# Expert steps in another order, and all weight subtractions in them on VectorE

## The chip, the cores and the metric

The kernel runs on one core of a Trainium2 chip. The metric is the device time of one launch in microseconds (us), as the median of three runs.

## The reference

A transformer of three layers on 1024 tokens of 1024 features: neighbourhood attention, grouped-query attention, and a hybrid mixer, each followed by a mixture of 32 experts. The changed code computes the experts. Each token goes to two of 32 experts, and an expert is a gated product:

```python
def expert_block(args):
    xb, e = args
    return (jax.nn.silu(xb @ w_gate[e]) * (xb @ w_up[e])) @ w_down[e]
```

The hidden width of an expert is 512 in the first two layers (wide) and 256 in the third (narrow). All inputs are float32, and the results are scaled by the gate and added up per token.

## The kernel before

Each of the three layers ends with a stage that runs its 32 experts in turn, each for its first 128 tokens (class `Experts`). The work is cut into steps; a step is the product with one tile `R` of 1 MB of the weights. In a wide layer an expert has six: g0 and g1 are the gate's product (into `pj` in PSUM), g2 and g3 the up product (into `S`), d0 and d1 the second product (into `O` and `R` in PSUM). In the narrow layer a g step makes both gate and up halves of `pj` for half of the features, so an expert has g0, g1 and one d.

For float32 accuracy each product is made of three on rounded operands (`mm3`, lines 181 to 184): high times high, low times high, high times low. So a tile of weights is split before its use: `make` (line 2189) rounds it on ScalarE to `H` (line 2197) and subtracts on VectorE, or for every sixth tile on GpSimd, to get `L` (line 2198). `make` runs three steps ahead of the product; there are four buffers of `H` and `L`. When a tile is split, `load` (line 2154) has SyncE's queue fetch the tile ten places on into the same buffer; the ring has ten.

Around the products there are small pieces of work per expert, in the methods that the change moves:

- `tokens(e, g)`: four transpositions on TensorE of half of the gathered rows `X` (line 2217) into `tp`, then the two parts `xh` (ScalarE, line 196) and `xl` (VectorE, line 197); after the second half GpSimd issues the gather of a later expert's rows (line 2205).
- `silu(e)`: ScalarE, `a` from `pj` (line 2231). `gated(e)`: VectorE, `a` times the up product (line 2235).
- `hidden(e)`: the transpositions of `a` (line 2217), then `th` and `tl`.
- `done(e)`: VectorE scales the second product out of PSUM (line 2247, two instructions) and GpSimd scatters the rows to `y` (line 2248).

The order of all of it on every engine is written by hand: `run` goes through the list `seq` and calls `step`, within a manual schedule, so each engine executes its instructions in the order in which `step` issues them. In `seq` the second product of an expert stands within the first products of the next: in a wide layer g0, g1 of expert e, then d0, d1 of e - 1, then g2, g3 of e. `gated(e-1)` stands before g0 and `hidden(e-1)` before g1.

Of the kernel before, what the change touches and what calls it, by code (L numbers as in the profile page):

```python
# [22 lines left out]
P = 128  # L23
# [16 lines left out]
def constants():  # L40
    """Arrays that depend on shapes alone."""
# [54 lines left out]
def part(gen, n):  # L96
    """The next n steps of gen."""
    return islice(gen, n)


def mixed(main, side, nm, ns):
    """Both generators to their ends, ns steps of side spread over nm of main."""
    done = 0
    for i, _ in enumerate(main):
        want = (i + 1) * ns // nm
        while done < want:
            done += 1
            next(side, None)
        yield
    run(side)  # L110


def together(gens, n, apart):
    """Steps of up to n generators in turn, to the ends of all; one starts the given steps after another."""
# [9 lines left out]
# the pools of the tiles of the weights of the experts, in turn; the first two hold four other tiles before  # L124
# [11 lines left out]
class K:  # L136
# [19 lines left out]
    # ---------------------------------------------------------------- setup  # L156
# [17 lines left out]
    def log_exp(self, after):  # L174
        """The functions Ln and Exp together, from after the given instruction on."""
        with self.tc.issue_after(after.ins):
            self.nc.scalar.preload_act_table_set("natural_log_exp_and_others")

    # ---------------------------------------------------------------- products
# [6 lines left out]
    def split(self, raw, hi, lo):  # L186
        """hi <- raw rounded to float32r; lo <- the rest."""
# [4 lines left out]
    def evac_split(self, src, hi, lo, scale=None):  # L192
        """hi, lo <- the two parts of src * scale, src in PSUM."""
# [8 lines left out]
    def feature_major(self, src, t, scol, bcol, hh, hl, pool):  # L202
        """Columns t of hh, hl <- the transposed token tile src, scaled and shifted per feature, in steps."""
# [18 lines left out]
    # ---------------------------------------------------------------- modulation  # L222
    def condition(self, c, name):
        """silu(c) over partitions."""
# [4 lines left out]
    def first_rows(self, x, ca, w, b, scol, bcol, hh, hl, q, r, closed):  # L229
        """hh, hl <- the transposed x * s + t per feature, for t, s - 1 <- the first 2048 entries of silu(c) @ w + b.  # L230

        In a first step all that does not need these entries, then by tile; closed() ends the tiles of q."""
# [76 lines left out]
    def modulation(self, ca, w, b, mod, first, last, pool):  # L309
        """Entries 512 * first to 512 * last of mod (DRAM) <- silu(c) @ w + b, in steps, outside TensorE but for the sum over partitions."""  # L310
        nc = self.nc
        todo = [(n, k) for n in range(first, last + 1) for k in range(NK)]
        # the bias of one part comes within the next part
# [18 lines left out]
        def total(acc, n):  # L332
            """The sum over partitions, in steps."""
# [33 lines left out]
    # ---------------------------------------------------------------- between mixer and experts  # L367
    def load_out(self, lay, moe, queue):
        """The next loads for the output product of the mixer, as far as there is room."""
# [13 lines left out]
    def mixer_out(self, lay, x, ot, x1, h2, hi, pool, first, moe, done):  # L383
        """x1 <- norm(alpha * x + (1 + g1) * (o @ w_o)); h2 <- the modulated x1; routes it.

        done() is called when the tiles of the pool first are no longer needed."""
# [30 lines left out]
        # the modulated rows are z * (g * (1 + sc)) + (b * (1 + sc) + sh)  # L417
# [14 lines left out]
        # the router takes the rows before their norm: its weights for them, and what the mean and the shift come to  # L432
# [145 lines left out]
    def columns(self, lay, prev, scol, bcol):  # L578
        """Scale and shift of the normalised rows of layer prev into the input of the mixer of lay."""
# [9 lines left out]
    # ---------------------------------------------------------------- neighbourhood attention  # L589
    def na_tables(self):  # L590
        """DRAM: the bias table of each head with room around it for the masked positions."""
# [13 lines left out]
    def na_attention(self, hh, hl, w, tables, ot, start, started, side):  # L605
        """ot (DRAM, features x tokens) <- the attention of hh + hl (features x tokens) without its output product."""
# [19 lines left out]
        # the parts of the weights of the values lie where other tiles do later  # L626
# [48 lines left out]
        # the products for keys, then queries, of each pair of heads: 16 products in a row  # L675
# [8 lines left out]
        def weights(n, half):  # L684
            """One half of the features of the weights of product n: the high part; the low one of the half before."""
# [11 lines left out]
        def project(j):  # L697
            """Step j: half of the sum over features for half of the tokens of product j // 4."""
# [15 lines left out]
        def settle(lo):  # L714
            """The next head's part of a product that is done, out of PSUM: its high part; then its low part."""
# [33 lines left out]
        def bias(h, ty):  # L749
            """The biases and the mask of head h for windows of type ty."""  # L750
# [15 lines left out]
        def scores(i):  # L766
            """Window i % 4 of head i // 4: the exponentials of its two halves."""
# [118 lines left out]
    # ---------------------------------------------------------------- vectors and norms  # L886
    def row(self, pool, src, name, bufs=1):
        """A vector of DRAM on every partition."""
# [5 lines left out]
    def col(self, pool, src, name):  # L894
        """A vector of DRAM over partitions: element k * 128 + p at (p, k)."""
# [4 lines left out]
    def rsqrt(self, out, v, tmp):  # L900
        """out <- v ** -0.5 (columns), in steps."""
# [8 lines left out]
    def normal(self, out, z, s):  # L910
        """out <- (z - mean) / std over its row, in steps; s: 20 columns that start with the statistics of the halves."""
# [9 lines left out]
    # ---------------------------------------------------------------- mixture of experts  # L921
# [1594 lines left out]
```

## Time and profile before

| | us |
|---|---|
| median of 3 runs | 4152.44 (4148.66 to 4153.31) |
| span of the profiled execution | 4140.5 |
| first wide stage, first product to last scaling, about | 637.7 (726.4 to 1364.1) |
| second wide stage, about | 637.7 (2196.5 to 2834.2) |
| narrow stage, about | 326 (3720 to 4046) |

Of the profiled execution the span is recorded, from its first instruction to its last; its own total time is not recorded apart. The span is 11.9 us under the median. Times in the rows below are us from the start of the span, durations in us unless marked ns. In rows of engines a bracket tells how long the engine was idle before the instruction and what ended that.

### The profile page before, as it was taken

How to read it: one execution, taken by the hardware profiler on the slowest of the kernel's cores; microseconds unless marked ns; L12 is line 12 of the kernel's file. 1: busy time of each engine (PE TensorE's matmuls, PEld its weight loads, DVE VectorE, ACT ScalarE, POOL GpSimd, SP SyncE). 2: the span in 40 equal slices, each digit the busy share in tenths (PEclk: the TensorE clock that was granted, in tenths of full speed). 3: DMA queues.
4: the chain of work that ended last, by engine and by line, in shares of the span. 5: the costliest groups of instructions: out<-in, count | busy, mean ns of one | idle time of the engine just before them, and what ended most of it. 6: DMA issues, size and time to landing. Idle time of an engine off the chain costs nothing. (4 is left out here: it accounts for less than half of the span.)

```text
span 4140.5 us, 51186 instructions
## 1 busy us (share of the span) xinstructions
PE 3457.2 (83%) x17648; PEld 2802.6 (68%) x17648; DVE 3382.8 (82%) x5129; ACT 2293.8 (55%) x3295; POOL 1905.4 (46%) x1230
## 2 busy tenths in 40 slices
PE   5999876899989687999877999984899879769991
PEld 4777665777777476777666777773778767657771
DVE  6599979888888797999797888888465578788986
ACT  3377632666666455888425666664352266227772
POOL 2255425444554234868454445544412142257763
PEclk8999988999999898999998999997999999989996
DMA  8878753999998547434537999995210012649994
GB/s 268 227 147 161 169 165 131 326 346 347 349 342 292 185 134 245 134 118 128 163 130 282 341 337 345 350 346 193 67 39 1 19 56 71 197 154 325 337 347 186
DMA packets 554648, 880.10 MB, mean 213 GB/s; under 512 B 117167, under 2 KB 280623, under 8 KB 551312
## 3 DMA queue, kind: packets, MB, share of 16 engines
q1 hardware_dynamic: 477008, 745.90, 54.1%
q0 software_dynamic: 77376, 130.88, 10.5%
q8 instruction: 141, 2.31, 0.2%
q14 instruction: 123, 1.01, 0.1%
HBM read 791.89 MB, written 126.82 MB: 222 GB/s over the span
## 5 line engine op out<-in xcount | busy, mean ns | idle before, releaser
L2198 DVE TENSOR_TENSOR L<-R,H 128x2048 fp32r<-128x2048 f32 x394 | 1057.0, 2683 | 178.7 <-ACT H L2197 178.7
L2197 ACT ACTIVATE H<-R 128x2048 fp32r<-128x2048 f32 x480 | 918.3, 1914 | 86.8 <-PE S L184 69.5
L2205 POOL DMA_INDIRECT X<-h,slots x87 | 194.8, 2239 | 575.1 <-PE tp L2217 554.8
L2198 POOL TENSOR_TENSOR L<-R,H 128x2048 fp32r<-128x2048 f32 x86 | 398.3, 4632 | 104.4 <-ACT H L2197 95.0
L182 PE MATMUL pj<-H,xh 128*128 128x512 f32 x776 | 319.4, 412 | 2.5 <-ACT H L188 2.5
L183 PE MATMUL pj<-L,xh 128*128 128x512 f32 x776 | 307.1, 396 | 1.8 <-DVE L L189 1.8
L184 PE MATMUL pj<-H,xl 128*128 128x512 f32 x776 | 307.6, 396 | 0.0
L2248 POOL DMA_INDIRECT y<-O,slots x96 | 263.8, 2747 | 92.9 <-DVE O L2247 57.7
L360 POOL TENSOR_TENSOR macc<-macc,mw 128x512 f32<-128x512 f32 x182 | 237.5, 1305 | 72.6 <-ACT mw L356 63.1
L196 ACT ACTIVATE ph<-tp 128x512 fp32r<-128x512 f32 (+1 forms) x352 | 199.4, 567 | 115.5 <-PE tp L1225 102.3
L197 DVE TENSOR_TENSOR pl<-tp,ph 128x512 fp32r<-128x512 f32 (+1 forms) x352 | 224.7, 645 | 25.0 <-ACT ph L196 23.6
L196 ACT ACTIVATE xh<-tp 128x512 fp32r<-128x512 f32 x194 | 116.0, 599 | 189.1 <-PE tp L2217 146.4
L1209 DVE TENSOR_REDUCE st<-S 128x1 f32<-128x1024 f32 (+2 forms) x192 | 204.1, 1063 | 19.2 <-PE S L1515 16.2
L182 PE MATMUL S<-H,xh 128*128 128x512 f32 x512 | 204.7, 400 | 0.0
L184 PE MATMUL S<-H,xl 128*128 128x512 f32 x512 | 200.5, 392 | 0.0
L183 PE MATMUL S<-L,xh 128*128 128x512 f32 x512 | 200.3, 391 | 0.0
L196 ACT ACTIVATE th<-tp 128x512 fp32r<-128x512 f32 (+1 forms) x97 | 51.0, 526 | 249.2 <-PE tp L2217 248.1
L1225 PE MATMUL tp<-ident,E 128*128 128x128 f32 x1111 | 171.5, 272 | 0.5 <-DVE pl L197 0.5
L1236 PE MATMUL O<-ph,V 128*128 128x512 f32 (+1 forms) x352 | 162.9, 463 | 10.4 <-DVE U L1243 10.4
L184 PEld LDWEIGHTS pj<-H,xl 128*128 128x128 f32 x776 | 148.0, 191 | 33.5 <-DVE xl L197 0.7
L182 PEld LDWEIGHTS pj<-H,xh 128*128 128x128 f32 x776 | 149.1, 192 | 30.8 <-ACT H L188 2.8
L183 PEld LDWEIGHTS pj<-L,xh 128*128 128x128 f32 x776 | 149.0, 192 | 30.2 <-DVE L L189 2.1
(589 smaller groups left out, 10198.3 us busy)
## 6 DMA issues: line engine op xcount, KB each, us to landing
R<-moe_w_down SPq DMA_DIRECT2D x161, 1024.0 KB
R<-moe_w_up SPq DMA_DIRECT2D x127, 1024.0 KB
R<-moe_w_gate SPq DMA_DIRECT2D x126, 1024.0 KB
mw<-ada_w SPq DMA_DIRECT2D x160, 256.0 KB
R<-moe_w_gate SPq DMA_DIRECT2D x66, 512.0 KB
R<-moe_w_up SPq DMA_DIRECT2D x66, 512.0 KB
Y<-y SPq DMA_DIRECT2D x24, 1024.0 KB
mw<-w_mod SPq DMA_DIRECT2D x96, 256.0 KB
```

The costliest lines, as they stand in the source:

```text
L182: mm(out, ah, bh, start=first, stop=False)
L183: mm(out, ah, bl, start=False, stop=False)
L184: mm(out, al, bh, start=False, stop=last)
L196: nc.scalar.activation(hi, src, AF.Copy)
L197: nc.vector.tensor_sub(lo, src, hi.bitcast(F32))
L360: nc.gpsimd.tensor_add(acc, acc, W)
L1209: nc.vector.tensor_reduce(blk.st[:, a, 0:1], S[:, :n], axis=AX.X, op=ALU.max, negate=True)
L1225: nc.tensor.transpose(tp[:, a, :], blk.E[a][:, c * P:(c + 1) * P], self.ident)
L2197: self.nc.scalar.activation(hi, r, AF.Copy)
L2198: (engine or (self.nc.gpsimd if i % 6 == 5 and i < self.n - 4 else self.nc.vector)).tensor_sub(lo, r, hi.bitcast(F32))
L2205: return self.nc.gpsimd.indirect_dma_start(out=self.X[e % 3], out_offset=None, in_=self.h2d, in_offset=IOA(ap=i, axis=0), bounds_check=T - ...
L2248: ins = nc.gpsimd.indirect_dma_start(out=self.y, out_offset=IOA(ap=self.slots.bitcast(I32)[:, 1, e:e + 1], axis=0), in_=O, in_offset=None, ...
```

## The change

Four things, all within the experts' steps.

- `seq`: the first products of an expert are no longer split by the second product of another. In a wide layer g0 to g3 of expert e are followed by d0, d1 of e - 1; in the narrow layer g0, g1 of expert e by d of e - 2.
- The small pieces stand at other steps. Wide: `hidden(e-1)` and `done(e-2)` before g1, `tokens(e+1, 0)` before g2, `silu(e)` and `tokens(e+1, 1)` before g3, `gated(e)` before d1. So three steps lie between the up product and the transposition of `a`, where there was one, and three between that and the second product, where there was one. Narrow: `silu(e-1)`, `gated(e-1)`, `tokens(e+1, 0)`, `done(e-3)` before g0, `tokens(e+1, 1)` before g1, `hidden(e-1)` before d.
- All subtractions that `step` causes are VectorE's. Those of three tiles per layer that are made before the stage name GpSimd themselves and stay there.
- Comments and docstrings are taken out, which moves line numbers by two in this part (2198 becomes 2196, 2217 becomes 2215, 2235 becomes 2233).

```diff
-        for e in range(33):
-            down = [("d", e - 1, j) for j in range(self.NF // 2)]
...
-            self.seq += up[0] + (down if e else []) + up[1]
+        lag = 1 if self.FF == 512 else 2
+        for e in range(32 + lag):
+            if e < 32:
+                self.seq += [("g", e, j) for j in range(self.FF // 128)]
+            if e >= lag:
+                self.seq += [("d", e - lag, j) for j in range(self.NF // 2)]
...
-        (engine or (self.nc.gpsimd if i % 6 == 5 and i < self.n - 4 else self.nc.vector)).tensor_sub(lo, r, hi.bitcast(F32))
+        (engine or self.nc.vector).tensor_sub(lo, r, hi.bitcast(F32))
...
+    def wide(self, kind, e, j):
+        if kind == "g":
+            if j == 0:
+                self.acc[e] = [self.k.ps.tile([P, 512], F32, name=n, bufs=2) for n in ("pj", "S")]
+                if e == 1:
+                    self.gated(0)
+            elif j == 1:
+                if e:
+                    self.hidden(e - 1)
+                if e > 1:
+                    self.done(e - 2)
+            elif j == 2:
+                self.tokens(e + 1, 0)
+            else:
+                self.silu(e)
+                self.tokens(e + 1, 1)
+        else:
+            if j == 0:
+                if e == 31:
+                    self.done(30)
+                    self.hidden(31)
+                self.out[e] = [self.k.ps.tile([P, 512], F32, name=n, bufs=1) for n in "OR"]
+            elif e < 31:
+                self.gated(e + 1)
+
+    def narrow(self, kind, e, j):
+        if kind == "g":
+            if j == 0:
+                self.acc[e] = [self.k.ps.tile([P, 512], F32, name="pj", bufs=2)]
+                if e:
+                    self.silu(e - 1)
+                    self.gated(e - 1)
+                self.tokens(e + 1, 0)
+                if e > 2:
+                    self.done(e - 3)
+            else:
+                self.tokens(e + 1, 1)
+                if e == 1:
+                    self.hidden(0)
+        else:
+            if e > 29:
+                self.done(e - 1)
+            self.out[e] = [self.k.ps.tile([P, 512], F32, name=n, bufs=1) for n in "OR"]
+            if e == 29:
+                self.silu(31)
+                self.gated(31)
+            if e < 31:
+                self.hidden(e + 1)
...
+        (self.wide if self.FF == 512 else self.narrow)(kind, e, j)
```

Three places show the new order. First VectorE in the middle of a wide stage, one expert and its repetition's start, before:

```order
L2235 TENSOR_TENSOR a<-S,a 128x512
L2198 TENSOR_TENSOR L<-R,H 128x2048
L197 TENSOR_TENSOR tl<-tp,th 128x512
L2198 TENSOR_TENSOR L<-R,H 128x2048 x2
L197 TENSOR_TENSOR xl<-tp,xh 128x512
L2198 TENSOR_TENSOR L<-R,H 128x2048
L197 TENSOR_TENSOR xl<-tp,xh 128x512
L2247 SCALAR_TENSOR_TENSOR O<-O,slots,g_6750 128x512
L2247 SCALAR_TENSOR_TENSOR O<-R,slots,g_6750 128x512
L2198 TENSOR_TENSOR L<-R,H 128x2048
```

and after the change:

```order
L2233 TENSOR_TENSOR a<-S,a 128x512
L2196 TENSOR_TENSOR L<-R,H 128x2048 x2
L197 TENSOR_TENSOR tl<-tp,th 128x512
L2245 SCALAR_TENSOR_TENSOR O<-O,slots,g_6750 128x512
L2245 SCALAR_TENSOR_TENSOR O<-R,slots,g_6750 128x512
L2196 TENSOR_TENSOR L<-R,H 128x2048
L197 TENSOR_TENSOR xl<-tp,xh 128x512
L2196 TENSOR_TENSOR L<-R,H 128x2048
L197 TENSOR_TENSOR xl<-tp,xh 128x512
L2196 TENSOR_TENSOR L<-R,H 128x2048 x2
```

There are five subtractions of weights per expert before and six after; the scalings moved from behind the second `xl` to behind `tl`.

Second TensorE in a wide stage at the end of g1 (`pj` is the gate's product, `tp` a transposition, `O` and `R` the second product, `S` the up product), before:

```order
L184 MATMUL pj<-H,xl 128x512
L182 MATMUL O<-H,th 128x512
L183 MATMUL O<-L,th 128x512
L184 MATMUL O<-H,tl 128x512
L182 MATMUL R<-H,th 128x512
```

and after the change:

```order
L184 MATMUL pj<-H,xl 128x512
L2215 MATMUL tp<-ident,X_6569 128x128 x4
L182 MATMUL S<-H,xh 128x512
L183 MATMUL S<-L,xh 128x512
L184 MATMUL S<-H,xl 128x512
```

After g1 the second product of the expert before followed; now the transposition of the next tokens and the up product do.

Third VectorE in the narrow stage, one expert whose three tiles are all its own, before:

```order
L2235 TENSOR_TENSOR a<-pj,a 128x256
L197 TENSOR_TENSOR xl<-tp,xh 128x512
L2198 TENSOR_TENSOR L<-R,H 128x2048
L197 TENSOR_TENSOR tl<-tp,th 128x256
L2247 SCALAR_TENSOR_TENSOR O<-O,slots,g_32458 128x512
L2247 SCALAR_TENSOR_TENSOR O<-R,slots,g_32458 128x512
L2198 TENSOR_TENSOR L<-R,H 128x2048
L197 TENSOR_TENSOR xl<-tp,xh 128x512
L2198 TENSOR_TENSOR L<-R,H 128x2048
```

and after the change, one expert:

```order
L2233 TENSOR_TENSOR a<-pj,a 128x256
L197 TENSOR_TENSOR xl<-tp,xh 128x512
L2245 SCALAR_TENSOR_TENSOR O<-O,slots,g_32459 128x512
L2245 SCALAR_TENSOR_TENSOR O<-R,slots,g_32459 128x512
L2196 TENSOR_TENSOR L<-R,H 128x2048
L197 TENSOR_TENSOR xl<-tp,xh 128x512
L2196 TENSOR_TENSOR L<-R,H 128x2048
L197 TENSOR_TENSOR tl<-tp,th 128x256
L2196 TENSOR_TENSOR L<-R,H 128x2048
```

An expert without a subtraction on GpSimd has the same nine instructions before and after; the second of each pair of experts had one subtraction less on VectorE before.

## Rows read from the trace of the kernel before

**Rows 1.** windows: busy us (count) of PE, PEld, DVE, ACT, POOL, then clock, DMA share, GB/s

```profile
726.40:1364.10 637.70, 577.40 (x2681) 468.10 (x2680) 551.36 (x351) 425.78 (x317) 295.98 (x92) 1.00 0.91 328
...
3720.00:4046.00 326.00, 308.77 (x1459) 245.88 (x1459) 286.31 (x268) 229.31 (x219) 224.67 (x75) 0.98 0.97 336
```

**Rows 2.** timeline of TensorE, one wide expert: start, us, line, [idle before]

```profile
1004.10 0.66 PE L2217 MATMUL tp<-ident,a 128*128 128x128 f32 x4 [1.82 <-DVE a L2235]
...
1007.36 0.39 PE L182 MATMUL O<-H,th 128*128 128x512 f32 x1
...
1010.08 0.60 PE L2217 MATMUL tp<-ident,X 128*128 128x128 f32 x4
...
1019.21 0.39 PE L182 MATMUL pj<-H,xh 128*128 128x512 f32 x1
...
1023.91 0.66 PE L2217 MATMUL tp<-ident,a 128*128 128x128 f32 x4 [1.82 <-DVE a L2235]
```

**Rows 3.** timeline of GpSimd in the same stretch

```profile
996.66 4.63 POOL L2198 TENSOR_TENSOR L<-R,H 128x2048 fp32r<-128x2048 f32 x1
1001.45 2.88 POOL L2248 DMA_INDIRECT y<-O,slots  x1 [0.16 <-issue]
1014.16 2.18 POOL L2205 DMA_INDIRECT X<-h,slots  x1 [9.83 <-PE tp L2217]
```

**Rows 4.** timeline of VectorE in the same stretch

```profile
998.83 4.61 DVE L2198 TENSOR_TENSOR L<-R,H 128x2048 fp32r<-128x2048 f32 x1 [1.28 <-ACT H L2197]
1003.36 0.68 DVE L2235 TENSOR_TENSOR a<-S,a 128x512 f32<-128x512 f32 x1
1003.96 2.27 DVE L2198 TENSOR_TENSOR L<-R,H 128x2048 fp32r<-128x2048 f32 x1
1006.16 0.68 DVE L197 TENSOR_TENSOR tl<-tp,th 128x512 fp32r<-128x512 f32 x1
...
1015.37 0.68 DVE L197 TENSOR_TENSOR xl<-tp,xh 128x512 fp32r<-128x512 f32 x1
1015.97 0.74 DVE L2247 SCALAR_TENSOR_TENSOR O<-O,slots,g 128x512 f32<-128x512 f32 x1
1016.62 0.74 DVE L2247 SCALAR_TENSOR_TENSOR O<-R,slots,g 128x512 f32<-128x512 f32 x1
```

**Rows 5.** groups of 760 to 1300 us: xcount | busy us, mean ns | idle before

```profile
L2198 DVE TENSOR_TENSOR L<-R,H 128x2048 fp32r<-128x2048 f32 x136 | 376.1, 2765 | 66.3 <-ACT H L2197 66.3
```

**Rows 6.** waits (total us, times, longest): TensorE's, first and second wide stage; ScalarE's, first

```profile
PE tp L2217 <- DVE a L2235: 58.8, 32, 3.5
...
PE tp L2217 <- DVE a L2235: 58.5, 32, 3.3
...
ACT H L2197 <- PE S L184: 34.7, 60, 0.8
```

**Rows 7.** timeline of ScalarE, the same wide expert

```profile
1011.21 1.92 ACT L2197 ACTIVATE H<-R 128x2048 fp32r<-128x2048 f32 x1
...
1019.41 1.92 ACT L2197 ACTIVATE H<-R 128x2048 fp32r<-128x2048 f32 x1 [0.80 <-PE S L184]
```

**Rows 8.** windows as in rows 1: one wide expert, a stretch of it, the narrow stage

```profile
1010.00:1019.00 9.00, 9.00 (x46) 7.42 (x44) 7.45 (x7) 6.74 (x5) 4.71 (x2) 1.00 1.03 398
...
1002.30:1022.10 19.80, 18.00 (x84) 14.62 (x84) 17.39 (x12) 13.46 (x10) 9.67 (x4) 1.00 0.98 345
...
3760.00:3955.00 195.00, 189.82 (x911) 150.75 (x910) 183.16 (x170) 144.83 (x138) 154.06 (x50) 1.00 1.00 341
```

**Rows 9.** timeline of VectorE in the narrow stage

```profile
3800.02 0.68 DVE L197 TENSOR_TENSOR xl<-tp,xh 128x512 fp32r<-128x512 f32 x1
...
3809.80 0.68 DVE L197 TENSOR_TENSOR xl<-tp,xh 128x512 fp32r<-128x512 f32 x1
...
3819.77 0.67 DVE L197 TENSOR_TENSOR xl<-tp,xh 128x512 fp32r<-128x512 f32 x1
```

**Rows 10.** timeline of ScalarE late in the narrow stage

```profile
3966.93 1.92 ACT L2197 ACTIVATE H<-R 128x2048 fp32r<-128x2048 f32 x1 [1.30 <-DMA R<-moe_w_down]
```

More of the change, by code (lines that the diff above doesn't have):

```diff
@@ L2141, in __init__ @@
         self.NF = self.FF // P
+        lag = 1 if self.FF == 512 else 2
         self.seq = []
-        for e in range(33):
-            down = [("d", e - 1, j) for j in range(self.NF // 2)]
-            if e == 32:
-                up = [[], []]
-            elif self.FF == 512:
-                up = [[("g", e, 0), ("g", e, 1)], [("g", e, 2), ("g", e, 3)]]
-            else:
-                up = [[("g", e, 0), ("g", e, 1)], []]
-            self.seq += up[0] + (down if e else []) + up[1]
+        for e in range(32 + lag):
[3 more added lines that the diff above has]
+                self.seq += [("d", e - lag, j) for j in range(self.NF // 2)]
         self.n = len(self.seq)
@@ L2254, in step @@
         k = self.k
-        big = self.FF == 512
-        if kind == "g":
-            if j == 0:
-                self.acc[e] = [k.ps.tile([P, 512], F32, name=n, bufs=2) for n in ("pj", "S")[:1 + big]]
-                if e and big:
-                    self.gated(e - 1)
-                elif e:
-                    if e == 1:
-                        self.silu(0)
-                        self.gated(0)
-                    self.hidden(e - 1)
-                    if e > 1:
-                        self.done(e - 2)
-            elif j == 1:
-                if e and big:
-                    self.hidden(e - 1)
-                elif not big:
-                    self.tokens(e + 1, 0)
-                    if e == 0:
-                        self.tokens(1, 1)
-            if big and (j == 2 or e == 0 and j == 3):
-                self.tokens(e + 1, j - 2 if e == 0 else 1)
-                if e:
-                    self.done(e - 1)
-                elif j == 2:
-                    self.silu(0)
-        else:
-            if j == 0:
-                self.out[e] = [k.ps.tile([P, 512], F32, name=n, bufs=1) for n in "OR"]
-            if e < 31:
-                if big and j == 0:
-                    self.silu(e + 1)
-                elif big:
-                    self.tokens(e + 2, 0)
-                else:
-                    self.silu(e + 1)
-                    self.gated(e + 1)
-                    self.tokens(e + 2, 1)
+        (self.wide if self.FF == 512 else self.narrow)(kind, e, j)
         if self.made < i + 4:
@@ L2316, in run @@
             for i in range(self.n):
-                if self.seq[i] == ("d", 31, 0) and self.FF == 512:
-                    self.gated(31)
-                if self.seq[i] == ("d", 31, 0):
-                    self.hidden(31)
-                    if self.FF == 256:
-                        self.done(30)
                 self.step(i)
```

## Prediction

> **What bounds the kernel now.** I read the kernel by stages, and in each stage I looked for the wait that ends last. Three stages run the experts: two wide ones (layers 1 and 2, 1 MB tiles of weights, six per expert) and a narrow one (three tiles per expert). In a wide stage TensorE is busy for 91% of the time at the full clock of 2.4 GHz, the DMAs move 328 GB/s, VectorE is at 86% [rows 1]. No engine is full, so something waits in a circle. One expert takes 19.81 us, from one transposition of `a` on TensorE at 1004.10 to the next at 1023.91 [rows 2]. Within it TensorE runs without a pause from 1004.10 until the last product that starts at 1019.21; that group is twelve matmuls, and twelve take 2.72 us (1007.36 to 1010.08), so TensorE is done at 1021.93. It works 17.83 us and stands for 1.98 us; the profile prints 1.82 of these, since it models the end of the last matmul 0.16 late. What it waits for is `a`, the product of the two halves, made by VectorE.
>
> VectorE is late because of one instruction. GpSimd takes one weight subtraction in six, 4.63 us from 996.66 to 1001.29 [rows 3]. VectorE's next subtraction starts at 998.83 and takes 4.61 us, where the one after it takes 2.27 [rows 4]. It ends 2.15 us after GpSimd's, which is nearly the whole 2.27: beside GpSimd's subtraction VectorE's hardly gets on. Then only comes `a` (1003.36), and TensorE starts at 1004.10. The mean of VectorE's subtractions, 2765 ns against 2.27 us for an undisturbed one, tells the same for the whole stretch [rows 5]. TensorE's wait for `a` is 58.8 us in the first wide stage and 58.5 in the second, 32 times each [rows 6].
>
> **The change in the wide stages.** It takes 31 subtractions per stage off GpSimd (every sixth tile up to the last four) and gives them to VectorE, and it puts three steps between the end of the product and the transposition of `a`, and three between that and the second product.
> What VectorE then has per expert, from start to start in [rows 4]: six subtractions of 2.20 us (1003.96 to 1006.16), three low parts of transposed tiles of 0.60 (1015.37 to 1015.97), two scalings of the result of 0.65 (1015.97 to 1016.62), one multiplication of 0.60 (1003.36 to 1003.96): 13.20 + 1.80 + 1.30 + 0.60 = 16.90 us. TensorE has the same work as before, 17.83 us. So VectorE fits, with 0.93 us to spare.
> Whether the order lets it fit, I laid out by hand. Call the six steps g0 to g3, d0, d1; the transpositions now stand before g1, g2, g3. A step takes 2.72 us without a transposition, 3.26 with that of `a` (1004.10 to 1007.36) and 3.21 with one of `X` (half of 1010.08 to 1019.21 less 2.72) [rows 2]. The steps then start at 0, 2.72, 5.98, 9.19, 12.40, 15.11, and the next expert at 17.83. ScalarE's rounding of a tile starts 0.20 after a step without transposition (1019.41 against 1019.21) and 1.13 after one with it (1011.21 against 1010.08), and takes 1.92 [rows 2, 7]; VectorE's subtraction can start then. In order of its queue: subtraction of g0 2.14 to 4.34, low part 4.94, scalings 6.24, g1 8.44, low part 9.04, g2 11.24, low part 11.84, wait to 12.24, g3 14.44, wait to 14.52, d0 16.72, multiplication 17.32, d1 19.52, wait to 19.97, which is g0 again. The waits sum to 0.93. Each subtraction makes the tile that is used three steps on; the tightest is g3's, done at 14.44 and wanted at 17.83: 3.4 us to spare. The transposed `a` is ready at 4.94 and wanted at 12.40. So nothing on this path reaches TensorE, and an expert takes 17.83 us.
> Sum: 31 of the 32 waits go; the last expert keeps its own, since no step follows it. About 58 us as printed, plus 31 times the 0.16 of the modelled end, is 63 us per stage and 126 us for the two. The two indirect DMAs per expert that GpSimd still issues (2.88 and 2.18 us [rows 3]) have 17.8 us to fit into and cost nothing. The loads move from GpSimd's and VectorE's ends to VectorE's alone, so that SyncE's queue is held by one engine; a tile is freed at most two steps later than now, against ten tiles of room.
>
> **DMA in the wide stages.** One expert moves 345 GB/s times 19.80 us = 6.83 MB [rows 8]. In 17.83 us that needs 383 GB/s. The nearest rows: 345 GB/s is what is asked for now, no ceiling; in a stretch of 9 us in which loads were queued all the time, 398 GB/s went through [rows 8]. I take 398, since only that stretch has a full queue, and the DMAs then have 4% to spare; the low end, that 345 is all that is to be had over a long time, stays for the range. The Trainium skill, "DMA: Bandwidth & Descriptors", section Specifications, gives about 358 GB/s as the limit of one core's HBM traffic; that speaks against the change, and by it an expert would take 6.83 MB / 358 GB/s = 19.1 us, an estimate from that page. The 9 us at 398 GB/s already lie over it, but they are short.
>
> **The narrow stage.** VectorE's work is 9.78 us in an expert without GpSimd's subtraction, with no idle time (3800.02 to 3809.80), and 9.97 in one with it (3809.80 to 3819.77) [rows 9]. Afterwards each expert is of the first kind: 0.09 us less on average, 3 us in 32. But here the DMAs are at 100% with 341 GB/s over 195 us [rows 8], and late in the stage ScalarE waits for a load to land [rows 10]; the end is set by them and the bytes don't change. At the end the order has two scalings of a result, 1.3 us, before each of the last two second products, which costs up to 2.6 us where it is not hidden by the loads. Bounds: 3 us less to 3 us more; I take +1.
>
> **The sum.** The profiled span is 4140.5 us, and the median of the three times, 4152.4, lies 11.9 above it; its own time is not recorded, and I take it as the median. 4152.4 - 126 + 1 = 4027 us, with 4018 to 4036 for this case: a little clock or start-up gain at the low end, small new waits at the high end.
>
> **The rivals.**
> The DMAs become the bound of the wide stages. For it: 98% busy share now [rows 8]. Against it: the 398 GB/s, and what ScalarE's rounding waits for in these stages is TensorE, not a load [rows 6]. Price: at the middle of both ends, 371 GB/s, an expert takes 18.4 us, 0.6 more than forecast, 18 us over a stage, which the ring hides (ten tiles are some 30 us of work, of which I count 20 as lead): no loss. At 345 it takes 19.8 us, 2.0 more, 61 a stage less 20 of lead: 41 twice, 4109 us. It decides from about 370 GB/s downwards. Chance 0.09. By the 358 GB/s of the Trainium skill's page, "DMA: Bandwidth & Descriptors", it would be 1.25 us per expert, 39 a stage less 20 of lead: 19 twice, 4065 us, an estimate from that page.
> VectorE becomes the bound through waits that stay. Its subtractions now wait 66.3 us for ScalarE in 27 experts, 2.46 each [rows 5]. If all of that stayed beside 16.90 us of work, an expert would take 19.36 us, 0.45 less than now: 31 times that twice is 28 us, 4125 us. Against it: half of that waiting is the 1.28 before the disturbed subtraction [rows 4], and the layout leaves 0.93. Chance 0.05.
> Slower: GpSimd's indirect DMAs hold up VectorE as its subtraction does. Both are issued on the engine that blocked VectorE for its whole instruction. Then each expert adds 2.88 + 2.18 = 5.06 us to VectorE's 16.90: 21.96 us, 2.15 more than now, 62 times: 133 us, 4286 us. It turns into a loss once 2.9 of these 5.06 us block. Against it: the issue from 1001.45 to 1004.33 runs beside a subtraction that starts at 1003.96 and takes the usual 2.27 [rows 3, 4]. Chance 0.03. The Trainium skill, "SBUF — State Buffer", section Who interferes with whom, says that a VectorE instruction with two SBUF inputs contends with a GpSimd instruction that reads SBUF, and that whoever is first holds the port for its whole instruction; the subtraction's row agrees, the indirect DMA's does not show it.
> That the order does not come out as written can't be: it is written by hand, and the three orders shown have the steps where the change says.
>
> **How the numbers follow.** Forecast 0.82, DMA 0.09, VectorE 0.05, slower 0.03, anything else 0.01. The range holds the forecast's own 4018 to 4036, two more below for what the narrow stage may give, and of the DMA rival, which runs from the forecast to 4109, somewhat under the nearer half: 4016 to 4060. A measurement of this kernel tells about 0.2%, 8 us, from no change. All of the forecast and both rivals above it that end below 4152 are faster: 0.95; within 0.2% 0.02; slower 0.03.
>
> **What would show it.** Right: TensorE's wait for `a` gone from the wide stages except for one at the end; 17.8 us from one transposition of `a` to the next; no subtraction over 2.4 us there; DMAs at about 383 GB/s; the narrow stage as long as now within 3 us. Wrong: ScalarE waiting for loads in a wide stage (the first rival), TensorE waiting for the low part of a tile (the second), subtractions of 4 to 5 us beside an indirect DMA (the third), or the narrow stage longer by over 5 us, which would mean that VectorE without a pause there does not keep up.

## The result, and the profile after

The changed kernel takes 4030.41 us (median of four, 4022.41 to 4040.65), the kernel before 4152.88 in the same comparison: a ratio of 0.970, with an interval of 0.968 to 0.972. The profiled execution of after is one of the four; it took 4040.65 us, 1.85 more than its span.

By stages, from the first product to the last scaling, the two profiled executions compare as follows.

| stage | before, us | after, us | difference |
|---|---|---|---|
| first wide | 637.7 | 574.1 | -63.6 |
| second wide | 638.3 | 572.8 | -65.5 |
| narrow | 330.0 | 321.5 | -8.5 |
| all the rest | 2534.5 | 2570.6 | +36.1 |

In before the narrow stage runs from 3717.0 to 4047.0 by this measure, 4 us more than the rough bounds of [rows 1]. Of its -8.5, 5.3 us are no gain. In the new order TensorE transposes the second expert's rows `X` before the first product, and waits 4.42 us for them; so the first product, at which the stage is taken to start, comes 7.1 us after the first transposition of `X`, and 1.8 us in before. TensorE's start of the narrow stage in before, in after (two lines), and in the first experiment below, which keeps the old order:

```profile
3715.20 1.94 PE L2217 MATMUL tp<-ident,X 128*128 128x128 f32 x8 [7.18 <-DMA X<-h,first]
...
3617.04 1.94 PE L2215 MATMUL tp<-ident,X 128*128 128x128 f32 x8 [7.29 <-DMA X<-h,first]
3623.40 1.08 PE L2215 MATMUL tp<-ident,X 128*128 128x128 f32 x4 [4.42 <-DMA X<-h,first]
...
3636.88 1.94 PE L2217 MATMUL tp<-ident,X 128*128 128x128 f32 x8 [7.29 <-DMA X<-h,first]
```

From the first of these transpositions to the last scaling it is 331.8 us in before and 328.6 in after, 3.2 less, and all the rest is then 30.8 longer, not 36.1. In the wide stages 1.8 us lie between the two starts in both kernels.

The rows that answer to [rows 1] are windows of after over the first wide, second wide and narrow stage. Columns: length, busy us (count) of PE, PEld, DVE, ACT and POOL, granted clock, DMA share, GB/s.

```profile
731.10:1305.10 574.00, 571.00 (x2681) 470.47 (x2680) 544.16 (x382) 425.80 (x317) 149.08 (x61) 1.00 0.99 364
2146.00:2718.80 572.80, 570.17 (x2681) 469.87 (x2680) 544.25 (x382) 425.71 (x317) 150.01 (x61) 1.00 0.99 366
3624.10:3945.60 321.50, 310.43 (x1470) 246.54 (x1468) 307.74 (x284) 228.10 (x221) 124.23 (x60) 0.99 0.98 339
```

TensorE, 577 of 638 us busy before, is now busy for 571 of 574. VectorE makes 31 more instructions in the stage, yet is busy 7 us less: the 31 subtractions cost it less than the hold had. The timeline of TensorE in after, against [rows 2]: three transpositions of `a` in a row.

```profile
1016.20 0.60 PE L2215 MATMUL tp<-ident,a 128*128 128x128 f32 x4
1033.97 0.60 PE L2215 MATMUL tp<-ident,a 128*128 128x128 f32 x4
1051.77 0.60 PE L2215 MATMUL tp<-ident,a 128*128 128x128 f32 x4
```

An expert takes 17.77 to 17.80 us, and the bracket with the wait is gone. TensorE's wait in the first wide stage (total us, times, longest), against [rows 6]:

```profile
PE tp L2215 <- DVE a L2233: 1.5, 1, 1.5
```

VectorE's subtractions there (ns: shortest, median, longest), against [rows 5]:

```profile
L2196 DVE TENSOR_TENSOR L<-R,H x189: 2278/2291/2295, 733.6 to 1293.7; 128x2048 fp32r<-128x2048 f32 x189
```

One wait is left where there were 32, and of 189 subtractions none takes over 2.30 us.

### The profile page after: what moved, and what is told of

Its sections match the earlier page's. It is cut to its first block, busy times and chain, and to the rows that moved or that the text cites. A ratio compares the mean times of both kernels' runs of the same rounds, so it can differ in the third digit from the quotient of the medians.

```text
span 4038.8 us, 51205 instructions
## 1 busy us (share of the span) xinstructions
PE 3474.8 (86%) x17648; PEld 2834.4 (70%) x17648; DVE 3390.2 (84%) x5206; ACT 2290.1 (57%) x3295; POOL 1511.5 (37%) x1153
## 5 line engine op out<-in xcount | busy, mean ns | idle before, releaser
L2196 DVE TENSOR_TENSOR L<-R,H 128x2048 fp32r<-128x2048 f32 x471 | 1076.8, 2288 | 48.4 <-ACT H L2195 47.9
L2246 POOL DMA_INDIRECT y<-O,slots x96 | 254.9, 2656 | 621.2 <-DVE O L2245 600.9
L2203 POOL DMA_INDIRECT X<-h,slots x87 | 166.8, 1918 | 401.2 <-PE tp L2215 380.3
L197 DVE TENSOR_TENSOR pl<-tp,ph 128x512 fp32r<-128x512 f32 (+1 forms) x352 | 224.8, 645 | 25.7 <-ACT ph L196 24.2
L1225 PEld LDWEIGHTS tp<-ident,E 128*128 128x128 f32 x1111 | 139.1, 141 | 37.1 <-DVE pl L197 1.7
L1219 ACT ACTIVATE E<-S,st 128x1024 f32<-128x1024 f32 (+6 forms) x149 | 157.1, 1054 | 10.3 <-DVE st L1209 9.2
```

The costliest lines, as they stand in the source:

```text
L197: nc.vector.tensor_sub(lo, src, hi.bitcast(F32))
L1225: nc.tensor.transpose(tp[:, a, :], blk.E[a][:, c * P:(c + 1) * P], self.ident)
L2196: (engine or self.nc.vector).tensor_sub(lo, r, hi.bitcast(F32))
L2203: return self.nc.gpsimd.indirect_dma_start(out=self.X[e % 3], out_offset=None, in_=self.h2d, in_offset=IOA(ap=i, axis=0), bounds_check=T - ...
L2246: ins = nc.gpsimd.indirect_dma_start(out=self.y, out_offset=IOA(ap=self.slots.bitcast(I32)[:, 1, e:e + 1], axis=0), in_=O, in_offset=None, ...
```

## Experiments: which part of the change gives what

The change does two things, so I undid each. **First, only the subtractions move to VectorE; the order stays that of before.**

```diff
-        (engine or (self.nc.gpsimd if i % 6 == 5 and i < self.n - 4 else self.nc.vector)).tensor_sub(lo, r, hi.bitcast(F32))
+        (engine or self.nc.vector).tensor_sub(lo, r, hi.bitcast(F32))
```

> The kernel before in its old order; the one edit is that VectorE makes every subtraction of the steps. Theory A (GpSimd's subtraction, which holds VectorE's up, is the cause of TensorE's wait for a): most of the wait goes. In the layout by hand of the old order VectorE still comes about 0.4 us late to a, so a wide expert takes about 18.2 us rather than 19.8: 1.6 x 62 = 99 us less than before, some 30 us more than the full change, and TensorE's wait for a in a wide stage is about 12 us rather than 58. Theory B (the few steps between the up product and the transposition of a are the cause, whoever subtracts): a wide expert stays at 19.4 to 19.8 us, at most 25 us less than before. Narrow stage: 9.8 us per expert until loads end it, within 5 us of before.

Measured: 4060.26 us, ratio 0.978 (0.976 to 0.980). Wide stages 589.7 and 590.1 us, narrow 326.7. TensorE's timeline in a wide stage:

```profile
1000.60 0.66 PE L2217 MATMUL tp<-ident,a 128*128 128x128 f32 x4 [0.32 <-DVE a L2235]
1018.90 0.66 PE L2217 MATMUL tp<-ident,a 128*128 128x128 f32 x4 [0.33 <-DVE a L2235]
```

Its wait in the first wide stage (total us, times, longest):

```profile
PE tp L2217 <- DVE a L2235: 12.1, 32, 1.4
```

18.3 us per expert and 12.1 us of wait: theory A, nearly to the number. The stages give 48.0 + 48.2 + 3.3 = 99.5 us. The new order adds 15.6 and 17.3 us in the wide stages: it takes away the 0.5 us per expert that are left (18.3 against 17.8). To the narrow stage it adds nothing: from the first transposition of `X` to the last scaling this run takes 328.5 us, the full change 328.6.

**Second, the order moves, and GpSimd keeps every sixth subtraction.**

```diff
-        (engine or self.nc.vector).tensor_sub(lo, r, hi.bitcast(F32))
+        (engine or (self.nc.gpsimd if i % 6 == 5 and i < self.n - 4 else self.nc.vector)).tensor_sub(lo, r, hi.bitcast(F32))
```

> The new order, but GpSimd keeps every sixth subtraction. Theory A in its strong form (a held-up subtraction makes a late wherever it stands): VectorE's work per wide expert is 5 x 2.20 + 2.34 for what the held-up one takes longer + 1.80 + 1.30 + 0.60 = 17.0 us, and waits come on top: 19 us per expert or more, at least 70 us slower than the full change. Theory B (the steps between decide; the held-up subtraction then lies under three steps of cover): 17.8 us per expert, as in the full change, within 10 us of its time, with VectorE's long subtractions of 4.6 us still there and no TensorE wait for a.

Measured: 4151.34 us, ratio 0.999 (0.997 to 1.000). The order alone is worth nothing that a measurement tells from no change: wide stages 624.8 and 622.5 us, narrow 352.0, which is 22 more than before (27 from the first transposition of `X`). My layout by hand (theory B) was wrong. Theory A's numbers came out (19.5 us per wide expert on average, 121 us over the full change), but not its mechanism: in the first wide stage TensorE waits for `a` for 1.6 us in all, and for the low part of a tile 30.1 us, in eight pauses. Timelines of the first wide stage: ScalarE's `silu`, which marks the experts; two subtractions of VectorE, each followed in the list by GpSimd's beside it; TensorE at its pause:

```profile
1001.16 0.58 ACT L2229 ACTIVATE a<-pj 128x512 f32<-128x512 f32 x1
1018.93 0.59 ACT L2229 ACTIVATE a<-pj 128x512 f32<-128x512 f32 x1
1036.72 0.58 ACT L2229 ACTIVATE a<-pj 128x512 f32<-128x512 f32 x1
1060.88 0.59 ACT L2229 ACTIVATE a<-pj 128x512 f32<-128x512 f32 x1
...
1042.65 7.13 DVE L2196 TENSOR_TENSOR L<-R,H 128x2048 fp32r<-128x2048 f32 x1
...
1043.04 4.59 POOL L2196 TENSOR_TENSOR L<-R,H 128x2048 fp32r<-128x2048 f32 x1
...
1069.23 4.17 DVE L2196 TENSOR_TENSOR L<-R,H 128x2048 fp32r<-128x2048 f32 x1 [2.11 <-ACT H L2195]
...
1066.62 4.63 POOL L2196 TENSOR_TENSOR L<-R,H 128x2048 fp32r<-128x2048 f32 x1 [2.41 <-issue]
...
1049.85 0.79 PE L183 MATMUL pj<-L,xh 128*128 128x512 f32 x1 [3.82 <-DVE L L2196]
1050.44 0.63 PE L184 MATMUL pj<-H,xl 128*128 128x512 f32 x1
```

Windows behind TensorE's pause (columns as above):

```profile
1050.00:1055.00 5.00, 5.00 (x14) 3.83 (x15) 4.79 (x3) 0.00 (x0) 0.00 (x0) 0.52 0.81 299
1055.00:1060.00 5.00, 5.00 (x27) 4.15 (x26) 3.98 (x4) 3.82 (x4) 1.69 (x1) 1.00 1.03 394
```

Three experts come every 17.8 us and the fourth takes 24.2, again and again over the stage (the first of the three stands just ahead of these lines). I read it so: VectorE falls behind a little in each, until the three steps of cover are used up; what the rows show is that TensorE then stands for 3.82 us for the low part of a tile. That pause costs more than itself: TensorE's granted clock in the 5 us behind it is 0.52, the 1.2 GHz level, and matmuls take 0.63 us there, where they take 0.39 at the full clock. What I had mis-sized is the hold: VectorE's subtraction ends 2.15 us after GpSimd's in both pairs of rows (1049.78 against 1047.63, 1073.40 against 1071.25), so it costs whatever of GpSimd's 4.6 us is still to come, 1.9 to 4.9 us beyond the usual 2.27, and I had counted 2.34. In the first pair VectorE's row begins 0.39 us before GpSimd's, and still it is VectorE that waits; so starts as close as these don't tell which of the two is first, and can't bear out the prediction's sentence that the first one holds the port.

**Third, the same question for the narrow stage alone** (the full change, with GpSimd's sixth for `self.FF == 256` only).

```diff
-        (engine or self.nc.vector).tensor_sub(lo, r, hi.bitcast(F32))
+        (engine or (self.nc.gpsimd if self.FF == 256 and i % 6 == 5 and i < self.n - 4 else self.nc.vector)).tensor_sub(lo, r, hi.bitcast(F32))
```

> The change, with GpSimd taking every sixth subtraction in the narrow stage alone. If VectorE's 9.78 us per expert set the narrow stage after its first eight experts, these experts now come every 9.4 to 9.5 us and the stage is 3 to 5 us shorter, or not at all where the loads then end it. If a held-up subtraction costs as much there as GpSimd takes off, the period stays 9.8 and the stage is within 2 us of the full change. The wide stages are untouched: 17.8 us per expert.

Measured: 4054.81 us; wide stages 575.8 and 572.8, narrow 351.8, 30 more than in the full change. Neither expectation held: a held-up subtraction costs more than GpSimd takes off. Experts take 11.37 and 10.53 us in turn, where the old order had 9.97 and 9.78 [rows 9]. VectorE and GpSimd:

```profile
3703.24 6.82 DVE L2196 TENSOR_TENSOR L<-R,H 128x2048 fp32r<-128x2048 f32 x1
...
3703.29 4.61 POOL L2196 TENSOR_TENSOR L<-R,H 128x2048 fp32r<-128x2048 f32 x1
```

In this order the two start together, and VectorE gets on only when GpSimd is through. So the order depends on the other part of the change: it gives nothing, or a loss, while GpSimd subtracts. The moved subtractions give most of the gain by themselves.

## Experiments: what on GpSimd holds VectorE up

The full change, and GpSimd works on a tile of its own that nobody reads, filling it in the first wide stage and copying it in the second.

```diff
+        if self.FF == 512 and i % 6 == 5 and i < self.n - 4:
+            if self.lay == 0:
+                self.nc.gpsimd.memset(self.spare, 0.0)
+            else:
+                self.nc.gpsimd.tensor_copy(self.spare, self.spare)
...
```

> The change, and GpSimd works once per wide expert on a tile of 128 x 2048 of its own that nobody reads: in the first layer it fills it with zeros (nothing read from SBUF), in the second it copies it onto itself (read and written). VectorE makes all subtractions. If any work of GpSimd in SBUF holds VectorE up: long subtractions (4 us and more) and a period over 18.5 us in both wide stages. If only work that reads SBUF does: 17.8 us and subtractions of 2.3 us in the first, over 18.5 us in the second. If it was the subtraction's two inputs: 17.8 us in both.

GpSimd's order isn't written by hand and this work waits for nothing, so all of it ran in the first 74 us of the first stage and the first 128 us of the second; the comparison is therefore of these stretches, not of whole stages (575.5 and 605.4 us). This kernel ran once, as did the one with the ring of eight, both without low parts, and the one before on its second profile. The groups there, GpSimd's and VectorE's of the first and then of the second stage (ns: shortest, median, longest):

```profile
L2199 POOL MEMSET spare<- x31: 1805/1817/2246, 734.9 to 803.3; 128x2048 f32 x31
...
L2196 DVE TENSOR_TENSOR L<-R,H x22: 2273/2287/2293, 734.1 to 801.5; 128x2048 fp32r<-128x2048 f32 x22
...
L2201 POOL COPY spare<-spare x31: 1897/3837/4059, 2149.1 to 2268.1; 128x2048 f32<-128x2048 f32 x31
...
L2196 DVE TENSOR_TENSOR L<-R,H x30: 2273/3376/4456, 2151.7 to 2270.7; 128x2048 fp32r<-128x2048 f32 x30
```

31 fills, and no subtraction takes longer. 31 copies, and both sides wait for each other: a copy takes 1.90 us at its shortest and 3.84 in the middle of the range, a subtraction 3.38 rather than 2.29, up to 4.46, and the experts of that stretch come every 20.6 to 24.8 us. The second theory: work that reads SBUF holds VectorE's subtraction up, work that only writes doesn't. The Trainium skill, "SBUF — State Buffer", section Who interferes with whom, says just this of a VectorE instruction with two SBUF inputs, and these rows agree with it. VectorE's instructions with one of their inputs in PSUM, its low parts of transposed tiles and its scalings, were not held up: in the first wide stage before none takes over 0.75 us, though GpSimd subtracts 31 times; the scaling at 1016.62 [rows 4], 0.74 us, lies wholly beside this one:

```profile
1016.47 4.63 POOL L2198 TENSOR_TENSOR L<-R,H 128x2048 fp32r<-128x2048 f32 x1
```

## Experiments: how near the loads are

The prediction took 398 GB/s as the DMAs' reach. This run leaves out the low parts of the weights, so that only the loads can set the pace.

```diff
-        hi, lo = [self.hi.tile(list(r.shape), F32R, name=n) for n in "HL"]
+        hi, lo = self.hi.tile(list(r.shape), F32R, name="H"), None
         self.nc.scalar.activation(hi, r, AF.Copy)
-        (engine or self.nc.vector).tensor_sub(lo, r, hi.bitcast(F32))
...
```

The rest of the edit leaves the products with the low parts out.

> The change with the low parts of the weights left out in all three expert stages: no subtraction on VectorE and no product of the high part with the low one on TensorE, which leaves TensorE about 12.4 us per wide expert and ScalarE about 14.5. The loads then set the pace, and the run shows how much the DMAs can give. If 398 GB/s is to be had, as the prediction took: 6.83 MB / 398 GB/s = 17.2 us per wide expert. If the full change with its 364 to 384 GB/s is already at the end of it: 17.8 to 18.7 us, so no room left. If 345: 19.8 us. Narrow stage, 3.6 MB per expert: 9.1 us at 398, 10.4 at 346 GB/s.

`silu` of three wide experts in a row:

```profile
998.39 0.57 ACT L2229 ACTIVATE a<-pj 128x512 f32<-128x512 f32 x1
1016.75 0.57 ACT L2229 ACTIVATE a<-pj 128x512 f32<-128x512 f32 x1
1035.08 0.57 ACT L2229 ACTIVATE a<-pj 128x512 f32<-128x512 f32 x1
```

Windows in the first wide and the narrow stage:

```profile
850.00:1200.00 350.00, 268.70 (x1143) 204.16 (x1142) 76.16 (x115) 253.21 (x191) 38.71 (x39) 0.95 1.01 374
...
3650.00:3850.00 200.00, 148.43 (x632) 102.48 (x630) 64.97 (x110) 134.60 (x131) 34.80 (x35) 0.96 1.00 340
```

After the first few experts one takes 18.3 us: the loads give 374 GB/s, not 398, and the full change's 17.8 us is 0.5 faster than they can follow. Then it must live on the tiles loaded ahead. If so, a shorter ring shows it:

```diff
-RING = 1, 1, 1, 0, 0, 0, 1, 2, 2, 2
+RING = 1, 1, 1, 0, 0, 0, 1, 2
```

> The full change with a ring of eight tiles rather than ten, which takes two tiles, 5.6 us of loads, from the lead. If the wide stage lives on its lead (17.8 us per expert where the loads alone need 18.3, as the run without low parts showed), the lead of the ten tiles falls by about 14 us over the stage, and with eight it is used up before the end: the last ten experts or so come every 18.3 us and ScalarE waits for loads, 4 to 8 us per wide stage. If the loads keep up with 17.8 us: no change in the wide stages. The narrow stage: 10 to 12 us per expert from some four experts earlier on, 3 to 8 us more.

Wide stages 577.9 and 578.8 us (3.8 and 6.0 more), narrow 328.0 (6.5 more, of which 3.6 are left from the first transposition of `X`, since the first product comes earlier here). `silu` of two experts late in the first wide stage:

```profile
1121.88 0.58 ACT L2229 ACTIVATE a<-pj 128x512 f32<-128x512 f32 x1
1140.20 0.58 ACT L2229 ACTIVATE a<-pj 128x512 f32<-128x512 f32 x1
```

ScalarE's waits for loads in the first and in the second wide stage:

```profile
ACT H L2195 <- DMA R<-moe_w_up: 37.3, 21, 3.2
...
ACT H L2195 <- DMA R<-moe_w_up: 27.3, 15, 3.7
```

With eight tiles the last experts come every 18.3 us, and ScalarE waits for loads. With ten it never does: 31 times 0.5 us is what the ring just covers.

**The narrow stage's loads.** ScalarE's waits for them in the narrow stage of the full change, where [rows 10] had the first signs of it:

```profile
ACT H L2195 <- DMA R<-moe_w_up: 22.2, 17, 2.1
...
ACT H L2195 <- DMA R<-moe_w_down: 11.1, 12, 2.0
```

33 us in all, and some nine of the late experts take 10 to 11.8 us. I first made the rows of a load longer in memory only:

```diff
-                start(r[:, :, a], (gate, up)[a][e, j * 512:(j + 1) * 512].rearrange("(k p) f -> p k f", p=P))
+                start(r[:, :, a], (gate, up)[a][e, j * 512:(j + 1) * 512].rearrange("(p k) f -> p k f", k=4))
...
```

The rest of the edit, here and in the next one, puts the columns of `X` and the products in the matching order.

> The change, with one edit in the narrow stage: each partition of a gate or up tile is loaded as one contiguous row of 4 KB rather than four of 1 KB, and the columns of X are turned in the matching order, so that the product is the same. If the loads' short rows set the late experts of the narrow stage (10 to 11.8 us where VectorE needs 9.78): DMA rate there from about 350 to about 390 GB/s, the experts all come every 9.4 to 9.8 us, ScalarE's wait for loads of 33 us in this stage goes, and the stage is 8 to 12 us shorter. If it is the bytes that set them, rate and stage stay within 2 us.

Nothing was gained (4029.45 us; narrow 325.5, 4 more than in the full change; wait 31 us), but as a test of the packets it was empty: in SBUF the pieces were still of 1 KB, and the packets kept their size. So both ends:

```diff
-            r = raw.tile([P, 4, 2, 256], F32, name="R")
+            r = raw.tile([P, 2, 4, 256], F32, name="R")
...
-                start(r[:, :, a], (gate, up)[a][e, j * 512:(j + 1) * 512].rearrange("(k p) f -> p k f", p=P))
+                start(r[:, a], (gate, up)[a][e, j * 512:(j + 1) * 512].rearrange("(p k) f -> p k f", k=4))
...
```

> As the run with long rows in the narrow stage, but the gate and up halves of a tile now also lie one after the other in SBUF, so that a load's rows are 4 KB long at both ends (there the rows in SBUF had stayed 1 KB pieces). If the packets' size sets the rate (346 GB/s with 1465 bytes per packet in the narrow stage of the full change, 374 GB/s with 2315 bytes in its wide stage): about 370 GB/s late in the narrow stage, ScalarE's wait for loads falls from 33 us to under 5, all experts come every 9.4 to 9.8 us, and the stage is 8 to 12 us shorter than 321 to 325. If the rate is that of the bytes whatever their packets: 346 to 351 GB/s again and the stage within 2 us of 325.

The DMAs over 200 us of the narrow stage, in the full change:

```profile
DMA packets 49918, 68.61 MB, mean 343 GB/s; under 512 B 4636, under 2 KB 42722, under 8 KB 49905
```

With long rows in memory alone:

```profile
DMA packets 50074, 68.79 MB, mean 344 GB/s; under 512 B 4642, under 2 KB 42870, under 8 KB 50061
```

With long rows at both ends:

```profile
DMA packets 22996, 74.21 MB, mean 371 GB/s; under 512 B 4911, under 2 KB 4911, under 8 KB 22983
```

371 GB/s with less than half the packets, and ScalarE waits for no load any more. The stage is only 3.2 us shorter (318.3; 4025.64 us in all), not 8 to 12, since every expert from about the tenth on now takes VectorE's 9.78. The window of that run shows why:

```profile
3700.00:3920.00 220.00, 217.93 (x1035) 176.04 (x1033) 220.00 (x204) 162.15 (x156) 89.61 (x43) 1.00 0.96 356
```

VectorE has 220 us of work in 220. The same long rows in all stages, without and with the low parts (the run without them has the edits of both):

> The low parts of the weights are left out again, and every gate and up tile, wide ones too, lies in rows of 4 KB (narrow) or 8 KB (wide) at both ends. Without the long rows the loads set 18.3 us per wide expert (373 GB/s) and about 10.5 us per narrow one (340 GB/s). If the packets' size sets the rate there as well: under 18.0 us wide and about 9.5 us narrow. If the rate ends at about 375 GB/s whatever the packets: 18.3 us wide, and 9.6 us narrow.

> The full change with all gate and up tiles in long rows, wide ones too. The wide stage keeps 17.8 us per expert, since TensorE sets it, and the narrow one 9.8 after its first eight experts, since VectorE does: a narrow stage of about 318 us, 4021 to 4028 us in all, no more than 10 us from the full change. A gain over the long packets in the narrow stage alone would need wide experts under 17.77 us, which TensorE's work rules out.

Without the low parts: 17.5 us per wide expert at 391 GB/s and about 10.0 per narrow one at 357, so longer packets lift the rate in the wide stage too, and in the narrow one by less than expected. There 10.0 us is more than VectorE's 9.78, so the run with long packets, whose ScalarE waits for no load, seems to live on its ring in the narrow stage as well; no run with a shorter ring tests that. With the low parts: 4011.23 us, ratio 0.9665 (0.9645 to 0.9685), the lowest median of this study and some 10 us below what I expected. Its interval overlaps those of the full change (0.968 to 0.972) and of the run with long packets in the narrow stage alone (0.965 to 0.971), so it isn't shown to be faster than they are. Its stages (574.0, 572.9, 318.7) are only 3 us below those of the full change; the rest lies where the two kernels do the same (2555.7 against 2570.6 us in the profiles).

## Experiments: the parts that the change does not touch

> The kernel before once more, for a second profile of the parts that the change does not touch. If they differ from one execution to the next by the granted clock alone (the profile of before had 0.934, that of the full change 0.924): about 0.930 here, wide stages of 638 us again, and 2534 to 2570 us outside the expert stages. If the change lengthens what follows its stages: 2534 us here too, against 2550 to 2571 in the kernels with the new order.

Measured: 4144.54 us, wide stages 637.9 and 639.7, narrow 328.7, 2536.4 outside (before: 2534.5), clock 0.933. The old order with VectorE's subtractions has 2553.0 outside, the runs with the new order and all products 2549.7 to 2570.6, of which some 5 us are the later first product of the narrow stage. The expectation's second case came out: both profiles of before lie below all nine of changed kernels, by 8 us at the least with the later start taken off. Of the +36.1, 23.1 us lie in the hybrid mixer, 8.5 between the two wide stages and 4.7 before the first. Windows over the whole of it, before:

```profile
2834.80:3717.00 882.20, 693.92 (x4236) 575.35 (x4236) 608.18 (x1332) 350.77 (x707) 290.13 (x230) 0.89 0.26 83
```

After:

```profile
2718.80:3624.10 905.30, 712.92 (x4240) 593.46 (x4241) 609.64 (x1333) 351.41 (x708) 291.17 (x231) 0.86 0.26 83
```

And in the run that gives GpSimd its sixth in the narrow stage alone:

```profile
2716.90:3604.80 887.90, 691.86 (x4241) 572.87 (x4241) 608.65 (x1333) 351.50 (x708) 291.29 (x231) 0.89 0.27 85
```

The last two run the same code up to there, 17 us apart, with the granted clock at 0.86 and 0.89. The last is 5.7 us longer than before, and 5.3 of these are the later first product, which ends this window: at 0.89 the mixer takes as long in both kernels. 300 to 350 us into this part the clock is 1.00 in both profiles of before, in the last of these runs and in those with the ring of eight and with long rows everywhere, and 0.73 to 0.77 in the six others with all products. After:

```profile
3018.80:3068.80 50.00, 49.40 (x370) 46.46 (x369) 19.51 (x51) 9.57 (x23) 3.81 (x3) 0.73 0.00 1
```

And the last of these runs again:

```profile
3016.90:3066.90 50.00, 49.41 (x511) 45.00 (x511) 28.66 (x83) 14.56 (x35) 8.43 (x9) 1.00 0.01 2
```

So of the +36 us some 17 go with the lower clock in the mixer of that execution and 5 with where the narrow stage is taken to start; the 13 in the first two layers are not traced to a cause. Whether a faster expert stage makes the lower clock behind it likelier is open: it did not occur in two profiles of before, and in six of nine of the changed kernels, one of them with the old order; that is too few to tell.

## Why the prediction was right, step by step

- **TensorE's 1.98 us per expert, and VectorE's held-up subtraction as its cause.** Right. The expert was to take 17.83 us and takes 17.78; the wait was to stay once per stage and does. The first run, with this cause alone removed, gives 100 us.
- **VectorE fits, with 0.93 us to spare, if the order is laid out by hand.** Right for the full change: its waits for ScalarE's rounding are 20.4 us in 31 experts, 0.66 each. The same kind of layout failed in the second experiment, since it gave a hold a fixed price, and the price depends on where the two engines meet.
- **GpSimd's indirect DMAs cost nothing.** Right: beside them no subtraction exceeded 2.30 us in the wide stages. The slower rival is out.
- **DMA.** The step that took 398 GB/s was wrong; the loads give 374 over 350 us, and nothing is to spare. The sign of 383 GB/s did not show: it was 364 and 366 over the wide stages, and 375 from 850 to 1200 us, which is what the loads can give. The prediction's rival had the right arithmetic for that: at 371 GB/s some 18 us are missing over a stage, and the ring hides them. It hides them with almost nothing left, as the ring of eight shows. By the 358 GB/s that the prediction quoted from the Trainium skill, 19.1 us per expert, the runs would have been slower than they are; the skill's page "HBM Reference", section Specifications (TRN2), has that figure for a core whose neighbour streams too, and says that a core streaming alone gets more.
- **The wide stages' sum.** 126 us forecast, 129.1 in the profiles.
- **The narrow stage.** +1 within ±3 us was forecast. The table's -8.5 is -3.2 from the first transposition of `X`. All of that comes from the subtractions (3.3 in the first run); it is what [rows 9] gave, 3 us in 32 experts, and the new order adds nothing. What failed is the step that struck these 3 us out because the loads set the end and their bytes don't change. ScalarE's waits for loads did grow, from 9.9 us in before to 33.3, yet the stage became shorter; VectorE was busy for 307.7 of 321.5 us, and what the loads could give hung on the packets, not on the bytes alone. That the 2.6 us of scalings at the end cost anything isn't shown by any run.
- **The base.** I took the profiled execution's own time as the median. With the 1.85 us of after it was about 4140.5 + 1.85 = 4142.4 us, 10 below it, and that of after is 10 above its median. The profiles differ by 101.7 us (132.3 gained in the stages from the first transposition of `X`, 30.8 lost outside), the medians by 122.5.

The mechanism of the wide stages, which is nearly all of the forecast, was right. That 4027 us came so near to 4030 is in part luck, by errors that cancel: 7 us more gained in the stages than the 125 summed up, and, if the stages are as long in the executions of the medians, some 10 lost outside them. That the loads fell short of 398 GB/s and cost nothing was a case that the prediction had only as a rival.

## What to carry to other kernels

Before work is shared between VectorE and GpSimd, look at the duration of VectorE's instruction beside GpSimd's: if it ends a fixed time after GpSimd's, the sharing can cost VectorE more than it takes off; here it did so in both orders. Give GpSimd work that does not read SBUF, or only issue DMAs from it. A stage that runs faster than its loads looks healthy as long as the ring lasts: compare its rate with a run in which the loads alone set the pace, and when they are short, make the rows of a load contiguous at both ends.

## What the runs showed of the hardware

- A subtraction on VectorE with both inputs in SBUF and a GpSimd instruction that reads SBUF exclude each other: 2.27 us became 4.2 to 7.1. A fill beside it cost nothing, and VectorE's scalings with one input in PSUM were not held up.
- The rate of loads depends on the packets: 343 GB/s with 1374 bytes on average, 371 with 3227 in the same stage; 374 and 391 in the wide stage without low parts. The length counts that is contiguous both in memory and in SBUF.
- A pause of TensorE of 3.8 us was followed by some 5 us at 1.2 GHz; the pauses of 1.8 us before the change [rows 2] were not, with the clock at 1.00 over the stage [rows 1].
